# One persistent ring of four weight tiles, and fixed places for the first FFN matmul's operands

## The chip, the cores and the metric

The kernel runs on one core of one Trainium2 chip. The metric is the device time of one execution in microseconds. The figure before is a median of three runs; the trace is of one further execution, taken with the hardware profiler.

## The reference, cut to what is computed

A trunk of two layers on a stream `h` of 1024 frames by 1024 channels, all in fp32. Layer 0 mixes by a gMLP, layer 1 by attention over a band of chunks. Each is followed by a squared-ReLU MLP with 4096 hidden channels, and both halves stand between two RMS norms.

```
for layer in range(DEPTH):                       # DEPTH = 2
    g = norm_g[layer]
    if layer < N_A_LAYERS:                       # layer 0
        m = gmlp_spatial_gating(rms_norm(h, g[0]), ...)
    else:                                        # layer 1
        k_band, v_band, valid = shared_kv_band(h, kv_norm_g, w_k, w_v)
        m = chunk_band_attention(rms_norm(h, g[0]), ...)
    h = h + rms_norm(m, g[1])
    f = sq_relu_mlp(rms_norm(h, g[2]), w_up[layer], w_down[layer])
    h = h + rms_norm(f, g[3])

def sq_relu_mlp(h, w_up, w_down):
    return jnp.square(jax.nn.relu(h @ w_up)) @ w_down
```

## The kernel before

**Precision.** Each fp32 matmul is made of three: a value is split into a high part H (a CAST by ScalarE) and a low part L (value minus H, a subtraction by VectorE), `split`, L112 to L117, and `mm3` (L135 to L138) issues H·H, H·L and L·H. So each weight block that TensorE (PE) multiplies goes first through one ScalarE (ACT) instruction at L116 and then one VectorE (DVE) instruction at L117.

**First FFN matmul.** `ffn` walks over 16 pairs of 128 hidden channels, j = 0 to 15. A pair's weights come in two raw tiles of 128x1024 (`load_pair`; up12r and up28r for j = 12), four 128x512 blocks b11, b21, b12, b22. Pairs 0 to 2 use plain products (`plain`). From j = 3 on `blocks` does seven products of 4·3 matmuls in the place of eight: b11·z11, t2·s2, b21·z12, t1·s1, t3·z21, t4·z22, b22·s4. Here t1 to t4 are sums of weight blocks, z11 to z22 the quarters of the normed stream and s1, s2, s4 sums of these. While block j multiplies, `Prep` (L521 to L550) makes the split operands of pair j+1 in six steps, which `blocks` calls at written places between the products. This part is under `tc.manual_schedule`: all engines run it in the order in which the code is written. So a row of ACT or DVE in this part waits for the one written before it, whatever it belongs to.

Between the steps, `blocks` turns products into results: the sums into `left.u` and `left.at(1)` (L576, L592, L593, L599, L606 on DVE), relu and square on ACT (`squared`, L446 and L447), five sums of the results on GpSimd (POOL; `sums`, L455), and the spill of them to DRAM (`spill`, L461, issued by SyncE, SP). The last of the DVE sums of a block, L606, with its relu, square and POOL sums, is kept back (`finish`) until the next block has begun. PE's last product of a block, b22·s4, adds into the PSUM tile that L593 has read; so b22·s4 can't start before L593 is done.

The split operands are tiles of a ring `u` with 8 places. The raw weight tiles are a ring of two (`raw`): the second raw tile of a pair takes the place that the last split of step 5 frees.

**Second FFN matmul.** Seven products p over eight steps jj (`operands`, `mms`). `operands(p, jj)` loads a tile `xr` of spilled results and one or two weight tiles `xw` and splits both: r or hlx, and dn or hlx (L685, with `halves`). Four of eight such tiles lie in a ring `w` of four, the other four in hlx. Here the order on each engine is a scheduler's. Before this matmul, the last block's `before.finish()` is called behind `operands(0, 0)`, and `before.spill()` at jj = 1.

**The rings in SBUF.** Each stage opens its own group of 8 KB weight tiles on the right side of SBUF, and closes it: l0w and l1w (`w` by 4) for the gMLP, the projections and the second layer's projection; up0 and up1 (`u` by 8, the same bytes) for the first FFN matmul; dn0 and dn1 (`w` by 4) for the second; and the attention's wq, wk, wv, and v2 by 2. The quarters of z lie in tiles a0 to a3, taken from a pool of their own.

## Time and profile before

| | us |
|---|---|
| median of 3 runs | 2229.82 |
| lowest and highest | 2229.69, 2232.67 |
| the profiled execution | 2224.22 |
| its span | 2222.5 |
| PE busy | 2151.9 (97%) |
| DVE, ACT, POOL busy | 1497.9, 1050.8, 596.5 |
| mean granted clock of PE | 0.99 |

The profiled execution is 5.6 us shorter than the median; 1.7 us of it lie outside the span. PE is busy nearly all the time, so the stages' time is PE's work, the stretches in which PE's clock is granted at half, and some 60 us in which PE waits. What a change off PE does is read from those waits: which engine ends them, and where. Times in the rows are us from the start of the span.

### The profile page before, as it was taken

Reading aid. Unit: us, or ns where it says so; the run is one execution under the profiler, and the core shown is the slowest. Engines: PE = TensorE matmul, PEld = TensorE weight load, DVE = VectorE, ACT = ScalarE, POOL = GpSimd, SP = SyncE. Lnnn points to the kernel's source line nnn. Section 1 sums busy time; section 2 is a strip of 40 time slices with the busy share of each in tenths; the row PEclk is TensorE's granted clock in tenths of the full one; section 3 lists DMA queues with packets and bytes.
Section 4 is the critical chain, followed back from the end, with each engine's and each line's share of the span. In section 5 each row is a group of like instructions: output and inputs, shape, how many; then the busy total and the mean of one; then the engine's idle time right before and its main releaser. Section 6 shows DMA issues by size and latency. Waiting matters only on the chain. (4 is left out here: it accounts for less than half of the span.)

```text
span 2222.5 us, 26708 instructions
## 1 busy us (share of the span) xinstructions
PE 2151.9 (97%) x9848; PEld 1744.8 (79%) x9848; DVE 1497.9 (67%) x2214; ACT 1050.8 (47%) x1755; POOL 596.5 (27%) x395
## 2 busy tenths in 40 slices
PE   8999999999999999989999999999999999999997
PEld 6888778777778888867888888777877777788786
DVE  6745187666656677767888888766956665664477
ACT  5333254444444444555566566654534444533342
POOL 1000010333333553461111111201023333444343
PEclk9999999999999999999999999999999999999998
DMA  4121342444467887831111111154334344877775
GB/s 171 44 80 61 117 175 86 162 135 139 157 240 274 285 301 247 277 133 50 51 51 41 51 50 50 63 185 146 110 137 133 138 156 163 323 259 262 270 261 213
DMA packets 113508, 347.01 MB, mean 156 GB/s; under 512 B 11360, under 2 KB 11360, under 8 KB 113376
## 3 DMA queue, kind: packets, MB, share of 16 engines
q1 hardware_dynamic: 112224, 341.11, 43.9%
q0 software_dynamic: 1152, 4.19, 0.6%
q8 instruction: 77, 1.26, 0.2%
q14 instruction: 55, 0.45, 0.1%
HBM read 261.89 MB, written 83.36 MB: 155 GB/s over the span
## 5 line engine op out<-in xcount | busy, mean ns | idle before, releaser
L697 POOL TENSOR_TENSOR xw<-xw,xw 128x1024 f32<-128x1024 f32 x80 | 212.2, 2654 | 284.2 <-DMA xw<-in_w_dn 269.6
L137 PE MATMUL pd<-hlx 128*128 128x512 f32 x448 | 176.2, 393 | 7.0 <-DVE hlx L117 7.0
L137 PE MATMUL pd<-dn,r 128*128 128x512 f32 x448 | 178.4, 398 | 3.7 <-DVE dn L117 3.7
L136 PE MATMUL pd<-dn,r 128*128 128x512 f32 x448 | 175.9, 395 | 2.5 <-ACT dn L116 2.5
L138 PE MATMUL pd<-dn,r 128*128 128x512 f32 x448 | 177.6, 396 | 0.0
L136 PE MATMUL pd<-hlx 128*128 128x512 f32 x448 | 175.5, 392 | 1.3 <-ACT hlx L116 1.3
L138 PE MATMUL pd<-hlx 128*128 128x512 f32 x448 | 175.6, 392 | 0.0
L136 PE MATMUL pu<-z,b 128*128 128x512 f32 x400 | 159.2, 398 | 1.8 <-ACT po L148 1.8
L138 PE MATMUL pu<-z,b 128*128 128x512 f32 x400 | 158.4, 396 | 2.6 <-DVE b L117 2.6
L137 PE MATMUL pu<-z,b 128*128 128x512 f32 x400 | 158.0, 395 | 0.0
L117 DVE TENSOR_TENSOR r<-xr,r 128x1024 fp32r<-128x1024 f32 x56 | 97.6, 1744 | 73.5 <-ACT r L116 73.4
L117 DVE TENSOR_TENSOR hlx<-xr,hlx 128x1024 fp32r<-128x1024 f32 x56 | 91.6, 1636 | 67.2 <-ACT hlx L116 67.0
L1015 ACT ACTIVATE p<-p,mn 128x640 f32<-128x640 f32 (+4 forms) x128 | 89.2, 697 | 58.6 <-DVE mn L1010 57.4
L116 ACT CAST tH<-ptr 128x512 fp32r<-128x512 f32 x192 | 80.8, 421 | 68.6 <-PE ptr L1033 66.2
L117 DVE TENSOR_TENSOR tL<-ptr,tH 128x512 fp32r<-128x512 f32 x192 | 92.2, 485 | 27.3 <-ACT tH L116 26.1
L116 ACT CAST hlx<-xr 128x1024 fp32r<-128x1024 f32 x56 | 58.8, 1050 | 106.0 <-DMA xr<-r 75.0
L137 PEld LDWEIGHTS pd<-hlx 128*128 128x128 f32 x448 | 84.6, 189 | 27.6 <-DVE hlx L117 9.5
L116 ACT CAST r<-xr 128x1024 fp32r<-128x1024 f32 x56 | 58.6, 1047 | 99.5 <-PE pd L138 59.6
L137 PEld LDWEIGHTS pd<-dn,r 128*128 128x128 f32 x448 | 85.9, 192 | 24.0 <-DVE dn L117 5.8
L136 PEld LDWEIGHTS pd<-dn,r 128*128 128x128 f32 x448 | 85.1, 190 | 21.6 <-ACT dn L116 3.4
L138 PEld LDWEIGHTS pd<-dn,r 128*128 128x128 f32 x448 | 85.9, 192 | 18.2
L136 PEld LDWEIGHTS pd<-hlx 128*128 128x128 f32 x448 | 84.7, 189 | 19.6 <-ACT hlx L116 1.7
(563 smaller groups left out, 6031.4 us busy)
## 6 DMA issues: line engine op xcount, KB each, us to landing
xw<-in_w_dn SPq DMA_DIRECT2D x192, 512.0 KB, 4.7
xr<-r SPq DMA_DIRECT2D x112, 512.0 KB, 4.6
r<-rx SPq DMA_DIRECT2D x48, 512.0 KB, 3.9
r<-r SPq DMA_DIRECT2D x48, 512.0 KB, 3.8
h<-h SPq DMA_DIRECT2D x24, 512.0 KB, 5.1
h<-in_x SPq DMA_DIRECT2D x16, 512.0 KB, 3.5
h<-m SPq DMA_DIRECT2D x16, 512.0 KB, 2.7
braw<-in_rel SPq DMA_DIRECT2D x16, 320.0 KB, 4.6
```

The costliest lines, as they stand in the source:

```text
L116: nc.scalar.copy(dstH, src)
L117: (eng_l or nc.vector).tensor_sub(dstL, src, dstH.bitcast(F32))
L136: nc.tensor.matmul(ps, aH, bH, start=first, stop=False, **kw)
L137: nc.tensor.matmul(ps, aH, bL, start=False, stop=False, **kw)
L138: nc.tensor.matmul(ps, aL, bH, start=False, stop=last, **kw)
L697: nc.gpsimd.tensor_tensor(ws[0], ws[0], ws[1], op=op)
L1015: nc.scalar.activation(pt[:, :w], pt[:, :w], AF.Exp, bias=mn, scale=-1.0, accum_out=sm)
```

## The change

Four 8 KB tiles, two of a tag `wa` and two of a tag `wb`, are laid once for the whole kernel between the quarters a0, a1 and a2, a3, in a group g0. They take the place of l0w, l1w, up0, up1, dn0, dn1, the attention's wq, wk, wv and one of its two v2. In the first FFN matmul the operands get fixed places in these tiles: b11 and t3 share one, b21 and t4 one, t2 and t1 one, and two generations of b22 one. `Prep`'s steps change with it: t2 is made at the end of step 1 (was: the start of step 2), t1 in step 3 (was t3), t3 in step 4 (was t4), t4 in step 5 (was t1). The first block (j = 3) runs steps 3 and 4 ahead of t2's product and step 5 behind it. In the last block, `operands(0, 0)` of the second matmul is issued inside `blocks`, ahead of the relu and square of L594, and `before.finish()` directly behind the block. The tags of the other stages follow.

```
+    ctx.enter_context(ph.group("g0", [("wa", [P, 2, D], 2), ("a0", QUAD, 1), ("a1", QUAD, 1),
+                                      ("wb", [P, 2, D], 2), ("a2", QUAD, 1), ("a3", QUAD, 1)]))
+    W4 = ("wa", "wa", "wb", "wb")
...
     def proj_first(src, w, m_dst):
-        units = [load_unit(w[0, kp], f"wo0{kp}") for kp in range(4)]
+        units = [load_unit(w[0, kp], f"wo0{kp}", W4[kp]) for kp in range(4)]
...
+        wt = [ph.t(W4[i], f"wt{i}", dt=F32R).rearrange("p a (s c) -> p a s c", s=2) for i in (0, 2, 1, 3)]
+        places = {n: wt[i][:, a] for i, ns in enumerate((("b11", "t3"), ("b21", "t4"), ("t2", "t1"), ("b220", "b221")))
+                  for a, n in enumerate(ns)}
+
         def operand(name, src):
-            u = ph.t("u", name, dt=F32R)
+            u = places[name]
             split(u[:, 0], u[:, 1], src)
             return u
...
                     self.make("b22", b22)
                     v(b12, b22, b12)
                     v(b22, b22, b11)
+                    self.make("t2", b22)
                 elif i == 2:
-                    self.make("t2", b22)
                     self.make("b21", b21)
                 elif i == 3:
                     v(b21, b22, b21)
+                    self.make("t1", b11)
+                elif i == 4:
                     self.make("t3", b12)
-                elif i == 4:
+                elif i == 5:
                     self.make("t4", b21)
-                elif i == 5:
-                    self.make("t1", b11)
...
             if first:
                 s3_in_place()
                 prep.step(3)
+                prep.step(4)
             else:
                 before.finish()
                 step(0)
             product(b2, w["t2"], s2, **part)
             v(left.u[:, 0], left.t1, b2, op=OP.add)
             if first:
-                prep.step(4)
                 prep.step(5)
...
             v(left.at(1), left.u[:, 1], b3, op=OP.add)
+            if nxt is None:
+                ahead.append(operands(0, 0))
             left.squared(1, 1)
...
                 before = blocks(prep, nxt, before)
                 prep = nxt
-        yield
+            before.finish()
...
-                rw = operands(p, jj)
-                if p == 0 and jj == 0:
-                    before.finish()
+                rw = ahead.pop() if ahead else operands(p, jj)
                 if p == 0 and jj == 1:
                     before.spill()
...
-                self.v = ph.t("v2", f"v{p}", [P, NT, 2, 2, 64], F32R)
+                self.v = ph.t("wb" if p % 2 else "v2", f"v{p}", [P, NT, 2, 2, 64], F32R)
...
-                                         tag="w" + kind, scale=cols[:, 1 if kind == "q" else 2])
+                                         tag="wb" if kind == "k" else "wa", scale=cols[:, 1 if kind == "q" else 2])
```

In the order of instructions the rows move at three places. (In the rows shown the changed kernel's lines L119 to L464 are the lines L116 to L461 of before; its L633 and L637 are L691 and L695.)

First, ACT in a block of the first matmul in layer 0 (block 8, which prepares pair 9). Before, b22 and t2 are the names b229 and t29, and r82 and r80 are results of block 8:

```order
300 L116 CAST b119_3662<-up9r_3633 128x512
301 L116 CAST b229_3679<-up25r_3635 128x512
302 L446 ACTIVATE r82_3640<-pu81_3642 128x512
303 L447 ACTIVATE r82_3640<-r82_3640 128x512
304 L116 CAST t29_3698<-up25r_3635 128x512
305 L116 CAST b219_3701<-up9r_3633 128x512
306 L116 CAST t39_3718<-up25r_3635 128x512
307 L446 ACTIVATE r80_3638<-r80_3638 128x512
308 L447 ACTIVATE r80_3638<-r80_3638 128x512
```

The changed kernel at the same place (wt0 to wt3 are the four shared tiles; wt3 holds b22, wt1 t2 and t1, wt2 b21):

```order
300 L119 CAST wt0_2357<-up9r_3594 128x512
301 L119 CAST wt3_2360<-up25r_3596 128x512
302 L119 CAST wt1_2359<-up25r_3596 128x512
303 L449 ACTIVATE r82_3601<-pu81_3603 128x512
304 L450 ACTIVATE r82_3601<-r82_3601 128x512
305 L119 CAST wt2_2358<-up9r_3594 128x512
306 L119 CAST wt1_2359<-up9r_3594 128x512
307 L449 ACTIVATE r80_3599<-r80_3599 128x512
308 L450 ACTIVATE r80_3599<-r80_3599 128x512
```

The CAST of t2 has moved ahead of the relu and square of r82, and so b21's CAST stands directly behind these; t1 has taken t3's turn.

Second, SP at the start of layer 0's second matmul. r07<-rx are the four spills of the last block, xr and xw loads of the second matmul. Before:

```order
154 L461 DMA r07_2341<-rx_2342 128x2x512 x2
155 L461 DMA r07_2341<-rx_2342 128x512
156 L691 DMA xr02_4839<-r02_2336 128x1024
157 L695 DMA xw020_4841<-in_w_dn 128x1024
158 L461 DMA r07_2341<-rx_2342 128x2x512
```

The changed kernel:

```order
152 L464 DMA r07_2352<-rx_2353 128x2x512
153 L633 DMA xr02_4747<-r02_2347 128x1024
154 L464 DMA r07_2352<-rx_2353 128x2x512
155 L464 DMA r07_2352<-rx_2353 128x512
156 L464 DMA r07_2352<-rx_2353 128x2x512
157 L637 DMA xw020_4749<-in_w_dn 128x1024
```

The load xw020 has moved behind the last spill of the block; xr02 has moved ahead of three of the spills.

Third, DVE at the start of layer 1's first matmul. b110 to b220 are the split operands of pair 0, m5 to m7 and z the end of the projection ahead of it. Before:

```order
1752 L142 TENSOR_SCALAR pri6_13322<-pss6_13320 128x1
1753 L209 TENSOR_TENSOR z32_12889<-ztr3_1_13305,z32_12889 128x4x128
1754 L213 SCALAR_TENSOR_TENSOR m6_13271<-m6_13271,pri6_13322,gpost_12901 128x1024
1755 L214 TENSOR_TENSOR m6_13271<-m6_13271,h6_13273 128x1024
1756 L142 TENSOR_SCALAR zri5_13331<-zss5_13329 128x1
1757 L197 SCALAR_TENSOR_TENSOR m5_13206<-m5_13206,zri5_13331,gnext_12903 128x1024
1758 L117 TENSOR_TENSOR b110_13389<-up0r_13385,b110_13389 128x512
1759 L117 TENSOR_TENSOR b210_13392<-up0r_13385,b210_13392 128x512
1760 L117 TENSOR_TENSOR b120_13395<-up16r_13387,b120_13395 128x512
```

The changed kernel, in which wt0 takes the high and low parts of pair 0's b11:

```order
1752 L145 TENSOR_SCALAR pri6_13214<-pss6_13212 128x1
1753 L212 TENSOR_TENSOR z32_12784<-ztr3_1_13197,z32_12784 128x4x128
1754 L216 SCALAR_TENSOR_TENSOR m6_13163<-m6_13163,pri6_13214,gpost_12793 128x1024
1755 L120 TENSOR_TENSOR wt0_13271<-up0r_13277,wt0_13271 128x512
1756 L217 TENSOR_TENSOR m6_13163<-m6_13163,h6_13165 128x1024
1757 L145 TENSOR_SCALAR zri5_13223<-zss5_13221 128x1
1758 L120 TENSOR_TENSOR wt1_13273<-up0r_13277,wt1_13273 128x512
1759 L120 TENSOR_TENSOR wt2_13272<-up16r_13279,wt2_13272 128x512
1760 L120 TENSOR_TENSOR wt3_13274<-up16r_13279,wt3_13274 128x512
```

The subtraction for pair 0's b11 has moved ahead of m6's addition and of m5's scaling, the other three ahead of m5's scaling.

## Rows read from the trace of the kernel before

**Rows 1.** The page's part 1: busy us, share, instructions of each engine.

```profile
PE 2151.9 (97%) x9848; PEld 1744.8 (79%) x9848; DVE 1497.9 (67%) x2214; ACT 1050.8 (47%) x1755; POOL 596.5 (27%) x395
```

**Rows 2.** Windows: stretch, length, busy PE, PEld, DVE, ACT, POOL; clock, DMA, GB/s.

```profile
428.53:628.12 199.59, 197.73 (x840) 156.86 (x840) 130.03 (x160) 93.24 (x160) 72.84 (x50) 1.00 0.44 148
1670.14:1869.96 199.82, 198.72 (x841) 157.01 (x841) 129.16 (x160) 93.24 (x161) 72.86 (x50) 1.00 0.43 145
650.70:660.70 10.00, 7.06 (x19) 5.24 (x19) 9.53 (x6) 6.08 (x8) 7.17 (x4) 0.66 0.90 315
1892.60:1899.80 7.20, 4.25 (x12) 3.10 (x12) 7.12 (x5) 5.12 (x7) 6.88 (x4) 0.76 0.91 318
1265.00:1272.00 7.00, 5.26 (x30) 4.33 (x29) 5.71 (x14) 3.75 (x11) 4.21 (x4) 1.00 0.19 75
```

**Rows 3.** Waits of PE in 415 to 640: us in total, times, longest.

```profile
PE pu L136 <- DVE r L593: 1.4, 6, 0.2
```

**Rows 4.** Timeline of ACT in a block: start, length, what, [idle before <-releaser].

```profile
556.72 0.63 ACT L447 ACTIVATE u<-u 128x512 f32<-128x512 f32 x1
557.26 0.60 ACT L116 CAST b<-up12r 128x512 fp32r<-128x512 f32 x1
559.54 0.62 ACT L116 CAST b<-up28r 128x512 fp32r<-128x512 f32 x1 [1.68 <-DMA up28r<-in_w_up]
560.07 0.59 ACT L446 ACTIVATE rx<-pu 128x512 f32<-128x512 f32 x1
560.69 0.63 ACT L447 ACTIVATE rx<-rx 128x512 f32<-128x512 f32 x1
...
563.54 0.62 ACT L116 CAST t<-up28r 128x512 fp32r<-128x512 f32 x1 [2.21 <-DVE up28r L540]
564.07 0.62 ACT L116 CAST b<-up12r 128x512 fp32r<-128x512 f32 x1
```

**Rows 5.** Timeline of DVE in the same block.

```profile
554.05 1.38 DVE L117 TENSOR_TENSOR t<-up11r,t 128x512 fp32r<-128x512 f32 x1 [1.87 <-ACT t L116]
...
559.61 1.36 DVE L536 TENSOR_TENSOR up12r<-up28r,up12r 128x512 f32<-128x512 f32 x1 [0.34 <-DMA up28r<-in_w_up]
...
564.80 0.69 DVE L117 TENSOR_TENSOR b<-up12r,b 128x512 fp32r<-128x512 f32 x1
...
567.44 0.69 DVE L593 TENSOR_TENSOR rx<-u,pu 128x512 f32<-128x512 f32 x1
```

**Rows 6.** Timeline of SP's queue in the same block: when the load was issued.

```profile
555.45 0.33 SPq L406 DMA_DIRECT2D up28r<-in_w_up  x1
```

**Rows 7.** Timeline of PE where four stages start or hand over.

```profile
651.97 1.20 PE L136 MATMUL pd<-dn,r 128*128 128x512 f32 x4 [1.23 <-ACT dn L116]
...
1497.86 0.50 PE L136 MATMUL po<-wo,o 128*128 128x512 f32 x1 [0.72 <-ACT ms L238]
...
1555.86 0.50 PE L138 MATMUL pu<-z,b 128*128 128x512 f32 x1 [2.55 <-DVE b L117]
...
1567.61 1.03 PE L193 MATMUL ztr<-ident,m 128*128 128x128 f32 x8
```

**Rows 8.** Timeline of DVE at the start of layer 1's first matmul.

```profile
1550.58 1.28 DVE L213 SCALAR_TENSOR_TENSOR m<-m,pri,gpost 128x1024 f32<-128x1024 f32 x1
...
1566.70 1.29 DVE L117 TENSOR_TENSOR b<-up1r,b 128x512 fp32r<-128x512 f32 x2 [0.52 <-ACT b L116]
```

**Rows 9.** Timeline at layer 0's second matmul: two rows of DVE, one each of POOL, SP.

```profile
651.38 1.22 DVE L117 TENSOR_TENSOR r<-xr,r 128x1024 fp32r<-128x1024 f32 x1
652.51 2.31 DVE L117 TENSOR_TENSOR dn<-xw,dn 128x1024 fp32r<-128x1024 f32 x1
...
655.92 2.26 POOL L455 TENSOR_TENSOR rx<-u,rx 128x512 f32<-128x512 f32 x1
...
658.20 0.37 SPq L461 DMA_DIRECT2D r<-rx  x1
```

**Rows 10.** The page's part 6: loads of xw, count, KB, median us to landing.

```profile
xw<-in_w_dn SPq DMA_DIRECT2D x192, 512.0 KB, 4.7
```

More of the change, by code (lines that the diff above doesn't have):

```diff
@@ L241, in proj_first @@
     def proj_first(src, w, m_dst):
-        units = [load_unit(w[0, kp], f"wo0{kp}") for kp in range(4)]
+        units = [load_unit(w[0, kp], f"wo0{kp}", W4[kp]) for kp in range(4)]
         ps = {}
@@ L267, in proj_second @@
         tail = Tail(zn, g_post, g_next, h_dst, first)
-        units = [load_unit(w[1, kp], f"wo1{kp}") for kp in range(4)]
+        units = [load_unit(w[1, kp], f"wo1{kp}", W4[kp]) for kp in range(4)]
         if rest is not None:
@@ L368, in run_ffn @@
         f = ffn(layer, *a)
-        before[0].__exit__(None, None, None)
-        with ExitStack() as dn:
-            with ph.group(f"up{layer}", [("u", [P, 2, 512], 8)], side="right"):
-                next(f)
-                next(proj, None)
-                before[1].__exit__(None, None, None)
-                dn.enter_context(ph.group(f"f{layer}", [("ps", [P, 512], 8)], **PS))
-                ph.live["tr"] = ph.live["ps"]
-                next(f)
-            dn.enter_context(ph.group(f"dn{layer}", [("w", [P, 2, D], 4)], side="right"))
+        next(f)
+        next(proj, None)
+        before.__exit__(None, None, None)
+        with ph.group(f"f{layer}", [("ps", [P, 512], 8)], **PS):
+            ph.live["tr"] = ph.live["ps"]
             for _ in f:
@@ L408, in load_pair @@
             return r
+        wt = [ph.t(W4[i], f"wt{i}", dt=F32R).rearrange("p a (s c) -> p a s c", s=2) for i in (0, 2, 1, 3)]
+        places = {n: wt[i][:, a] for i, ns in enumerate((("b11", "t3"), ("b21", "t4"), ("t2", "t1"), ("b220", "b221")))
+                  for a, n in enumerate(ns)}
         def operand(name, src):
-            u = ph.t("u", name, dt=F32R)
+            u = places[name]
             split(u[:, 0], u[:, 1], src)
@@ L528, in make @@
             def make(self, name, src):
-                self.w[name] = operand(f"{name}{self.j}", src)
+                self.w[name] = operand(name + str(self.j % 2) if name == "b22" else name, src)
             def step(self, i):
@@ L540, in step @@
                     v(b22, b22, b11)
+                    self.make("t2", b22)
                 elif i == 2:
-                    self.make("t2", b22)
                     self.make("b21", b21)
@@ L571, in blocks @@
                 prep.step(3)
+                prep.step(4)
             else:
@@ L593, in blocks @@
             v(left.at(1), left.u[:, 1], b3, op=OP.add)
+            if nxt is None:
+                ahead.append(operands(0, 0))
             left.squared(1, 1)
@@ L611, in blocks, with halves, operands, plain_operands @@
             return left
-        def plain_operands(j, src):
+        made, hlx, ahead = [0], {}, []
+        def halves(raw, name):
+            n = made[0] % 8
+            made[0] += 1
+            i = n // 2
+            if n >= 4 and i not in hlx:
+                hlx[i] = quad(i, f"hlx{i}", F32R)
+            d = ph.t(W4[n], name, [P, 2, T], F32R) if n < 4 else hlx[i][:, n % 2 * 2:n % 2 * 2 + 2]
+            split(d[:, 0], d[:, 1], raw)
+            return [d[:, i].rearrange("p (a c) -> p a c", a=2) for i in range(2)]
+        def operands(p, jj):
+            place, terms, op, _ = PRODUCTS[p]
+            raw = ph.t("raw", f"xr{p}{jj}")
+            nc.sync.dma_start(raw, r_dram[jj][:, place * T:(place + 1) * T])
+            ws = []
+            for i, (kh, dh) in enumerate(terms):
+                ws.append(ph.t(wtags[i % len(wtags)], f"xw{p}{jj}{i}"))
+                nc.sync.dma_start(ws[-1], wdn[kh, dh, jj])
+            if op is not None:
+                nc.gpsimd.tensor_tensor(ws[0], ws[0], ws[1], op=op)
+            return halves(raw, f"r{p}{jj}"), halves(ws[0], f"dn{p}{jj}")
+        def plain_operands(src, names):
             b11, b21, b12, b22 = src
-            w = [operand(f"b11{j}", b11), None, operand(f"b21{j}", b21), None]
-            w[1], w[3] = operand(f"b12{j}", b12), operand(f"b22{j}", b22)
-            return w
+            w = [operand(n, x) for n, x in zip(names, (b11, b21, b12, b22))]
+            return [w[0], w[2], w[1], w[3]]
+        own = ("t3", "t1", "t4", "b220"), ("b11", "t2", "b21", "b221")
         with tc.manual_schedule(engines=ALL):
-            w0 = plain_operands(0, load_pair(0))
+            w0 = plain_operands(load_pair(0), own[0])
         yield
@@ L673, in ffn @@
                 prep = nxt
[L674 removed]
+            before.finish()
         acc = [quad(i, f"acc{i}", F32) for i in range(2)]
[L676 to L698 removed]
         def mms(ps, tt, jj, rw):
@@ L725, in ffn @@
             for jj in range(n):
-                rw = operands(p, jj)
-                if p == 0 and jj == 0:
-                    before.finish()
+                rw = ahead.pop() if ahead else operands(p, jj)
                 if p == 0 and jj == 1:
@@ L828, in gmlp @@
             v_tile(0, t, units)
-        units = [load_unit(io["w_inv"][1, kp], f"wv1{kp}", tag="w" if kp else "x") for kp in range(4)]
+        units = [load_unit(io["w_inv"][1, kp], f"wv1{kp}", tag=W4[kp] if kp else "x") for kp in range(4)]
         for t in range(NT):
```

80 lines of the change are left out of this document (28 added, 52 removed).

## The prediction

> **What bounds the kernel now.** I read the page's first part, then windows, then the waits and timelines of the places that the change touches. PE is busy 97% of the span [rows 1]: the reader is to see that nothing which saves work off PE saves time unless PE waits for it. So the question is where PE waits, and who ends the wait.
>
> In blocks 4 to 14 of the first FFN matmul, the longest stretch that the change touches, PE is busy 197.73 of 199.59 us in ten blocks of layer 0 and 198.72 of 199.82 in layer 1 [rows 2]. That is one block in 19.96 and 19.98 us, of which PE idles 0.19 and 0.11. It idles always at one place, ahead of b22·s4, for DVE's L593 [rows 3]. So a loop that doesn't contain PE has the same period as PE, to 0.2 us. The loop can be followed in one block. Step 5's last split, 554.05 + 1.38, frees a raw tile [rows 5]; the load of up28r is issued at 555.45 [rows 6]; DVE's L536 starts at 559.61, let go by that load [rows 5]; from there ACT and DVE hand each other the splits until L593, 567.44 to 568.13 [rows 4, 5]; behind L593 come the relu and square, and steps 4 and 5 with the next such split. No row of ACT or DVE on this path waits for PE: ACT waits for DVE, for a DMA and for L540. The loop runs by itself, and has no slack to give.
>
> **The change part by part.**
>
> *The order in Prep's steps.* ACT's wait of 2.21 us ahead of t2's CAST, for L540 [rows 4], is now filled with the relu and square of the running block (560.07, 560.69). The change puts t2's CAST ahead of them, as the two ACT listings show. They can't start before L540 is done then, and b21's CAST, which followed t2's by 0.53 (563.54 to 564.07), follows behind them. Starts on ACT: CAST to relu 0.53 (559.54 to 560.07), relu to square 0.62 (560.07 to 560.69), square to CAST 0.54 (556.72 to 557.26), together 1.69 [rows 4]. b21's CAST comes 1.69 - 0.53 = 1.16 later. DVE's subtraction for it started 0.73 behind the CAST's start (564.07 to 564.80), 0.11 more than the CAST's 0.62 [rows 4, 5], I suppose because DVE was still busy; it won't be now, so between 1.05 and 1.16 reach DVE. I take 1.08. From that subtraction to L593 DVE's rows stand back to back, 564.80 to 567.44 = 2.64 [rows 5], and their number and form stay (t1's low part for t3's). So L593 comes 1.08 later in each block; nothing else of the loop gets shorter, since step 5 still ends with a split from the same raw tile and the load still waits for it. The period becomes 21.04 in layer 0. The eleven blocks 4 to 14 prepare a next one: 11 x 1.08 = **+11.9 us**. In layer 1 the loop stands 0.08 nearer to PE's own period (0.11 idle for 0.19), so I take 1.0: 11 x 1.0 = **+11.0**. Upper end 22 x 1.16 = +25.5. The cover of the old order was ACT's 2.21 us wait; with it gone, nothing else hides the two instructions. Lower end: nothing, if the loop doesn't hold PE (a rival). Each block then has a wait of some 1.3 us ahead of b22·s4.
>
> *The start of layer 0's second matmul.* PE waits there 1.23 us for dn's CAST [rows 7]; in the window 650.70 to 660.70 it idles 10.00 - 7.06 = 2.94 in all, and the granted clock is 0.66, which costs another 0.34 x 10 = 3.4 [rows 2]. The change issues r00 and dn00 before the block's end, beside t4·z22 and b22·s4, and could remove most of 6.3. But xw020 now stands on SP behind the last spill of the block (SP listings). That spill waits for POOL's last sum, 655.92 + 2.26, and went at 658.20 [rows 9]; with the relus and squares behind the CASTs of r00, dn00 and r01 I put it at some 660. The load takes 4.7 [rows 10], the subtraction 1.22 [rows 9] and the CAST ahead of it about as much, so dn02 is there at 667 at the earliest. PE, without its first waits, would be through jj = 0 and 1 (2 x 24 matmuls of 197.73 / 840 = 0.235 [rows 2], 11.3 us) at 651 + 11.3 = 662.3. It waits 4 to 6 us at jj = 2, and the clock falls again. Before, with 6.3 lost, it came there at 650.7 + 6.3 + 11.3 = 668.3. So the gain is given back: between -6 (xw020 in time) and +6 (the longer wait costs clock twice); I take **+2**.
>
> *The start of layer 1's second matmul.* The same waits: idle 7.20 - 4.25 = 2.95, clock 0.76, 0.24 x 7.2 = 1.7, in all 4.65 [rows 2]. Here xw020 stands ahead of the spills. I keep 0.3 of wait for dn00: **-4.3**, between -4.65 and -2.
>
> [...] The row first: a subtraction of 128x1024 takes 1.22 in one row and 2.31 in the next, around POOL's sums [rows 9]. [...] The splits of r00 and dn00 move among POOL's sums of the last block. [...]
>
> *The start of layer 1's first matmul.* PE waits 2.55 for b11's low part [rows 7], which stood on DVE behind m6's and m5's instructions. Now it follows L213, which ends at 1550.58 + 1.28 = 1551.86 [rows 8], so it is there at some 1552.5, when PE is. The next pair's splits at 1566.70 [rows 8] move only some 0.6 earlier, and PE, which came to them behind the transposes at 1567.61 + 1.03 [rows 7], would come 2.55 earlier: up to 0.6 of the gain is lost there. **-2.0**, between -2.55 and 0.
>
> *The projection ahead of it.* wo1's tiles now share wa with two of wo0, and are filled only when those are read. PE's wait there is 0.72 now [rows 7]; I estimate **+1.0**, between 0 and +2 (a load's 4.7 [rows 10] less what the remaining tiles cover).
>
> *The rest.* Block 3's steps and the attention's shared tags move loads and splits whose next use lies later than the move; +0.3 in all, between -2 and +2.
>
> Sum: 11.9 + 11.0 + 2 - 4.3 - 2.0 + 1.0 + 0.3 = **+19.9 us**. On the profiled execution that is 2224.2 + 19.9 = 2244.1. The median of the runs lies 5.6 above it; the same difference on the median gives 2249.7, and I forecast 2250.
>
> **The rivals.** (1) *The loop doesn't hold PE.* If PE paces the loop (L593 waits for PE's own sums, say, by an amount under what the rows resolve), 1.08 is paid once in each layer: 2.2 - 3.0 of the rest = -0.8, 2229. For it: PE's idle in the blocks is under 1% [rows 2]. Against: DVE runs without a break into L593, and the wait is there in more than half of the blocks. (2) *The same, and xw020 comes in time.* Then layer 0's start gives -6: 2.2 - 3.0 - 8 = -8.8, **2221**, faster. It decides by whether the spill goes before 655, since the load and the split then end by 662. Against: POOL's last sum starts no earlier than before. (3) *Each new wait makes the clock fall.* A fall as in the window at 1892.60 costs 1.7 [rows 2]; a block that runs late by 1.7 has no wait at b22·s4, so about every second block pays, part of it inside the loop's slack: +5 to +37, 2255 to 2287. Against: the window 1265 to 1272 holds 1.74 us of idle PE and its clock is 1.00 [rows 2]. [...] (4) *The change doesn't do what it says*: the shared tiles could make a CAST of one operand wait for PE's reading of its neighbour in the tile. b11's CAST would then wait for t3·z21, some 8 us in a block (from 557.26 to just ahead of L592 and L593 [rows 4, 5]), and the time would go beyond 2300. The order gives b11's CAST no PE to wait for; I hold it for very unlikely.
>
> **How the numbers follow.** The forecast has 0.70, rival 1 0.10, rival 2 0.12, rival 3 0.06, rival 4 0.02. With the terms at their lower ends together (17 - 6 - 4.65 - 2.55 - 2, with 17 from 0.78 a block, if the loop has 0.3 of slack that the rows don't show) the forecast's case reaches +2; at its upper ends (25.5 + 6 - 2 + 0 + 2 + 2) +33. Ends don't meet, so +9 to +29 holds most of it. To hold 8 in 10 the range takes in rival 1's neighbourhood and a part of rival 3: 2231 to 2262, the forecast's own being 2239 to 2259. A measurement of this kernel can tell about 0.2%, 4.5 us. Faster: rival 2 and a tail, 0.13. Same: rival 1 and the forecast's lowest ends, 0.12. Slower: 0.75.
>
> **What would show it.** Right: PE waits near 1.3 us ahead of b22·s4 in blocks 4 to 14, ended by L593, the period 21.0; ACT's relu of the running block directly behind t2's CAST; no wait of PE at layer 1's two starts; in layer 0 a wait at jj = 2 behind xw020. Wrong: a period that stays at 20.0, or b21's CAST that comes no later. The half clock inside the blocks would bear out rival 3; a wait of ACT for PE at b11's CAST rival 4.

## The result, and the profile after

The changed kernel is slower: 2246.15 us, median of six runs (2243.9 to 2249.81), against 2230.01 before (2229.69 to 2232.67, six runs). The ratio is 1.0071, with an interval of [1.0058, 1.0084]: 16.1 us more. The profiled execution took 2244.61, its span is 2242.8; that of before took 2224.22. So the two profiles stand 20.4 apart and the medians 16.1, because the profile of before lies 5.8 below its median and that of after 1.5.

The first part of the page of after (busy time, share of the span, instructions), which answers to [rows 1]:

```profile
PE 2133.7 (95%) x9848; PEld 1748.3 (78%) x9848; DVE 1510.0 (67%) x2214; ACT 1049.1 (47%) x1755; POOL 598.2 (27%) x395
```

PE has 18 us less of busy time than before, with the same number of matmuls, in a span that is 20 longer. Two things have happened, in opposite directions, and only one of them was forecast.

Stretches of after: from:to, length, busy PE (matmuls), PEld, DVE, ACT and POOL, clock, DMA share, GB/s. The first two run over ten blocks, from the last product of block 4 to that of block 14, in layers 0 and 1, and answer to the ten-block windows of [rows 2]. The next two, called the starts of the second FFN matmul below, hold the last block and the first 96 matmuls of the second FFN matmul, and the last lies in the gMLP:

```profile
425.11:635.92 210.81, 196.07 (x840) 157.01 (x840) 130.87 (x160) 93.10 (x160) 72.82 (x50) 1.00 0.42 140
1687.52:1898.93 211.41, 196.95 (x841) 159.16 (x841) 130.81 (x160) 92.92 (x161) 72.73 (x50) 0.98 0.41 137
635.92:686.58 50.66, 46.42 (x192) 37.10 (x193) 25.04 (x23) 24.72 (x31) 14.25 (x10) 0.97 0.68 241
1898.93:1944.22 45.29, 45.29 (x192) 37.29 (x193) 24.55 (x21) 22.93 (x30) 15.23 (x10) 0.96 0.69 244
100.00:260.00 160.00, 159.99 (x774) 134.29 (x774) 69.43 (x75) 50.93 (x67) 2.24 (x4) 1.00 0.24 75
```

The last three of them in the trace of before, the same pieces of work (the gMLP window is the same time):

```profile
628.12:678.63 50.51, 47.57 (x192) 37.99 (x193) 27.42 (x23) 24.49 (x32) 15.83 (x10) 0.93 0.76 268
1869.96:1919.23 49.27, 46.33 (x193) 37.05 (x193) 27.03 (x23) 24.04 (x31) 16.79 (x11) 0.97 0.76 267
100.00:260.00 160.00, 160.00 (x761) 131.94 (x760) 68.74 (x77) 49.23 (x65) 3.75 (x5) 1.00 0.21 68
```

The reader is to see three things. A block of the first matmul now takes 21.08 and 21.14 us, for 19.96 and 19.98. The start of the second matmul is 4 us shorter in layer 1 and no shorter in layer 0. And in the gMLP, whose order of work did not change, PE does 774 matmuls in 160 us where it did 761.

Cut at PE's instructions, the two profiles differ so (us, after less before):

| stretch | before | after | difference | forecast |
|---|---|---|---|---|
| start to layer 0's first FFN matmul | 313.01 | 308.27 | -4.7 | 0 |
| layer 0, block 3 to block 14 | 221.08 | 233.53 | +12.5 | +11.9 |
| layer 0, start of the second matmul | 50.51 | 50.66 | +0.2 | +2 |
| start of the attention | 28.5 | 31.6 | +3.1 | 0 |
| layer 1, projection | 54.73 | 55.59 | +0.9 | +1.0 |
| layer 1, first matmul to block 3 | 96.20 | 96.29 | +0.1 | -2.0 |
| layer 1, block 3 to block 14 | 221.17 | 234.59 | +13.4 | +11.0 |
| layer 1, start of the second matmul | 49.27 | 45.29 | -4.0 | -4.3 |
| the rest | | | -1.1 | +0.3 |
| sum | | | +20.4 | +19.9 |

**One block after.** ACT, start, length, what, [idle before <-releaser]; block 12 of layer 0, which answers to [rows 4]. The CASTs are b22's (584.10), t2's (588.04), and b21's together with t1's (589.73); L449 and L450 are the relu and square of the running block:

```profile
584.10 0.62 ACT L119 CAST wt<-up29r 128x512 fp32r<-128x512 f32 x1 [1.84 <-DMA up29r<-in_w_up]
588.04 0.62 ACT L119 CAST wt<-up29r 128x512 fp32r<-128x512 f32 x1 [3.32 <-DVE up29r L543]
588.57 0.59 ACT L449 ACTIVATE r<-pu 128x512 f32<-128x512 f32 x1
589.19 0.63 ACT L450 ACTIVATE r<-r 128x512 f32<-128x512 f32 x1
589.73 1.12 ACT L119 CAST wt<-up13r 128x512 fp32r<-128x512 f32 x2
```

DVE behind it, which answers to [rows 5]; the three rows are the low parts of t2 and b21, and L596 (L593 of before):

```profile
588.70 0.69 DVE L120 TENSOR_TENSOR wt<-up29r,wt 128x512 fp32r<-128x512 f32 x1 [0.74 <-ACT wt L119]
590.36 0.69 DVE L120 TENSOR_TENSOR wt<-up13r,wt 128x512 fp32r<-128x512 f32 x1 [0.98 <-ACT wt L119]
...
593.02 0.69 DVE L596 TENSOR_TENSOR r<-u,pu 128x512 f32<-128x512 f32 x1
```

And PE's b22·s4, with the waits of PE in 415 to 640 (us in total, times, longest), which answer to [rows 3]:

```profile
593.76 0.50 PE L139 MATMUL pu<-s,wt 128*128 128x512 f32 x1 [1.54 <-DVE r L596]
```

```profile
PE pu L139 <- DVE r L596: 8.1, 6, 1.5
PE pu L139 <- DVE rx L596: 7.1, 5, 1.4
```

From t2's CAST to b21's it is 589.73 - 588.04 = 1.69, the 1.69 that the prediction summed from ACT's starts, where it was 0.53. From b21's subtraction to L596 it is 593.02 - 590.36 = 2.66 (forecast 2.64). PE waits 15.2 us in eleven blocks, 1.4 each, always at this place.

### The profile page after: what moved, and what is told of

It is laid out like the page before. It is cut to its first block, busy times and chain, and to the rows that moved or that the text cites. A ratio compares the mean times of both kernels' runs of the same rounds, so it can differ in the third digit from the quotient of the medians.

```text
span 2242.8 us, 26750 instructions
## 1 busy us (share of the span) xinstructions
PE 2133.7 (95%) x9848; PEld 1748.3 (78%) x9848; DVE 1510.0 (67%) x2214; ACT 1049.1 (47%) x1755; POOL 598.2 (27%) x395
## 5 line engine op out<-in xcount | busy, mean ns | idle before, releaser
L639 POOL TENSOR_TENSOR xw<-xw,xw 128x1024 f32<-128x1024 f32 x80 | 218.1, 2727 | 274.3 <-DMA xw<-in_w_dn 247.5
L139 PE MATMUL pu<-z,wt 128*128 128x512 f32 x608 | 239.2, 393 | 2.4 <-ACT po L151 2.3
L141 PE MATMUL pu<-z,wt 128*128 128x512 f32 x608 | 237.3, 390 | 0.9 <-DVE wt L120 0.9
L140 PE MATMUL pu<-z,wt 128*128 128x512 f32 x608 | 238.0, 391 | 0.0
L140 PE MATMUL pd<-dn,r 128*128 128x512 f32 x448 | 174.9, 390 | 0.3 <-DVE dn L120 0.3
L139 PE MATMUL pd<-dn,r 128*128 128x512 f32 x448 | 175.0, 391 | 0.0
L141 PE MATMUL pd<-dn,r 128*128 128x512 f32 x448 | 174.8, 390 | 0.0
L139 PE MATMUL pu<-s,wt 128*128 128x512 f32 x312 | 128.6, 412 | 43.8 <-DVE rx L596 24.7
L139 PEld LDWEIGHTS pu<-z,wt 128*128 128x128 f32 x608 | 114.9, 189 | 28.1 <-ACT po L151 2.6
L141 PEld LDWEIGHTS pu<-z,wt 128*128 128x128 f32 x608 | 114.6, 189 | 25.8 <-DVE wt L120 1.3
L140 PEld LDWEIGHTS pu<-z,wt 128*128 128x128 f32 x608 | 114.8, 189 | 23.8
L141 PE MATMUL pu<-s,wt 128*128 128x512 f32 x312 | 126.0, 404 | 3.6 <-DVE wt L120 3.6
L140 PE MATMUL pu<-s,wt 128*128 128x512 f32 x312 | 125.8, 403 | 0.0
L120 DVE TENSOR_TENSOR dn<-xw,dn 128x1024 fp32r<-128x1024 f32 x56 | 89.4, 1596 | 42.6 <-ACT dn L119 42.1
L120 DVE TENSOR_TENSOR hlx<-xw,hlx 128x1024 fp32r<-128x1024 f32 x56 | 89.0, 1589 | 35.6 <-ACT hlx L119 35.4
L139 PEld LDWEIGHTS pu<-s,wt 128*128 128x128 f32 x312 | 60.5, 194 | 66.6 <-DVE rx L596 29.8
```

The lines of the kernel that those rows point to most:

```text
L120: (eng_l or nc.vector).tensor_sub(dstL, src, dstH.bitcast(F32))
L139: nc.tensor.matmul(ps, aH, bH, start=first, stop=False, **kw)
L140: nc.tensor.matmul(ps, aH, bL, start=False, stop=False, **kw)
L141: nc.tensor.matmul(ps, aL, bH, start=False, stop=last, **kw)
L639: nc.gpsimd.tensor_tensor(ws[0], ws[0], ws[1], op=op)
```

## The experiments

The lines of the changed kernel are three higher than those of before in `split` and `blocks` (L596 is L593).

### Does the place of t2 cost the time of the blocks?

First the change with t2 put back to the start of step 2, all else left:

```
                     v(b22, b22, b11)
-                    self.make("t2", b22)
                 elif i == 2:
+                    self.make("t2", b22)
```

> The changed kernel with one line moved back: t2 is made at the start of step 2 again, so on ACT the relu and square of the running block stand ahead of t2's CAST; ring, fixed places and early operands(0, 0) stay. Theory A (the order in Prep is the cost): the period of blocks 4 to 14 falls from 21.1 back to 20.0, 22 blocks by 1.1 to 1.2 = 25, time 2246 - 25 = 2221 (2217 to 2225), below the kernel before. Rival B (the cost lies in the shared tiles or in the moved steps 3 to 5): the period stays near 21 and the time above 2240.

Measured: 2218.53, ratio 0.995 [0.9934, 0.9966], faster than before by 12 us and than the change by some 27. Then the other way round: the kernel before, with nothing but t2 at the end of step 1.

```
                     v(b22, b22, b11)
-                elif i == 2:
                     self.make("t2", b22)
+                elif i == 2:
```

> The kernel before with that one line alone: t2 at the end of step 1. Theory A: 22 x 1.08 to 1.16 = 24 to 26 more than before, 2254 to 2256, with PE waiting 1.2 ahead of b22*s4 in each block. Rival B: no change, 2230.

Measured: 2253.49, ratio 1.0104 [1.0087, 1.0122], 22.6 us slower. The ten blocks of layer 0, the window of t2 put back first, then that of t2 alone:

```profile
425.04:624.63 199.59, 196.19 (x840) 156.98 (x840) 129.60 (x160) 93.24 (x160) 72.79 (x50) 1.00 0.44 148
```

```profile
431.45:642.29 210.84, 197.78 (x840) 156.88 (x840) 130.97 (x160) 93.06 (x160) 72.80 (x50) 1.00 0.42 140
```

The one line moves the block from 19.96 to 21.08 and back, in either kernel. That settles the main term: the rest of the change neither causes nor needs it. It also leaves a gain of some 12 us in the rest of the change, more than the prediction had there.

### Why is PE faster in the gMLP?

Start to start, the 128x512 matmuls of the two products with z take a median of 227 ns there, for 233 to 234 before (the window holds smaller matmuls too). The ring stood between the quarters now, so the first theory (L) was the ring's place. The experiment lays the ring behind all four quarters:

```
-    ctx.enter_context(ph.group("g0", [("wa", [P, 2, D], 2), ("a0", QUAD, 1), ("a1", QUAD, 1),
-                                      ("wb", [P, 2, D], 2), ("a2", QUAD, 1), ("a3", QUAD, 1)]))
+    ctx.enter_context(ph.group("g0", [("a0", QUAD, 1), ("a1", QUAD, 1), ("a2", QUAD, 1), ("a3", QUAD, 1),
+                                      ("wa", [P, 2, D], 2), ("wb", [P, 2, D], 2)]))
```

> The changed kernel with the four tiles laid behind all four quarters of z instead of between them; nothing else differs. In the trace after the change PE runs 774 matmuls in 100 to 260 us, before 761. Theory L (the pace comes from where the tiles lie): here 761 again, the first FFN matmul starts some 5 us later (313 for 308), and the rest of layer 1's projection too; the blocks are held by the loop, so little there: 2246 + 5 to 10 = 2251 to 2256. Rival: the pace comes from something else in the change (which tiles are shared, the order of splits): 774 stays, 2246.

Measured: 2248.52, ratio 1.0083 [1.0062, 1.0105], and in the gMLP window still 774 matmuls:

```profile
100.00:260.00 160.00, 160.00 (x774) 134.37 (x773) 69.46 (x75) 50.94 (x67) 3.56 (x5) 1.00 0.23 74
```

The time alone does not tell this run from the change, whose interval overlaps; the count does. The theory fell. What the ring does have in both places is the start address of its tiles: by the layout of the programs they stand alike with the quarters modulo 256 bytes of a partition, and in the kernel before they do not. No profile shows an address, so the differences given here are read from the layout, and what the runs vary is the pads. Three pads of 32 bytes, between ring and quarters, undo that, and move the tiles behind them as well:

```
+    pad = [P, 8]
+    ctx.enter_context(ph.group("g0", [("wa", [P, 2, D], 2), ("pad0", pad, 1), ("a0", QUAD, 1), ("a1", QUAD, 1), ("pad1", pad, 1),
+                                      ("wb", [P, 2, D], 2), ("pad2", pad, 1), ("a2", QUAD, 1), ("a3", QUAD, 1)]))
...
```

> The changed kernel with three pads of 32 bytes a partition between the ring's tiles and the quarters of z, so that the ring starts at a multiple of 64 bytes and the quarters (and all tiles behind them) at 32 more; nothing else differs. In the traces so far matmuls whose two operands start alike modulo 64 bytes follow each other at 227 ns, others at 232 to 234 (before: ring at 32, z at 0). Theory M (the pace comes from this): the window 100 to 260 holds 761 matmuls again in the place of 774, the first FFN matmul of layer 0 starts at some 313 in the place of 308, and with the projection of layer 1 and the plain blocks the time is 2246 + 7 to 11 = 2253 to 2257. Rival (the pace comes from the tiles' distance or order): 774 and 2246.

Measured: 2255.83, ratio 1.0123 [1.0103, 1.0144], 10 us slower than the change, and 760 matmuls in the window:

```profile
100.00:260.00 160.00, 160.00 (x760) 132.11 (x759) 68.36 (x76) 49.29 (x65) 2.79 (x5) 1.00 0.21 68
```

The other way round, the kernel before with one pad of 32 bytes under its right side, which makes ring and quarters alike modulo 64:

```
+    ctx.enter_context(ph.group("g1", [("padr", [P, 8], 1)], side="right"))
+    ph.t("padr", "padr")
```

> The kernel before with one pad of 32 bytes at the top of the right side, so that its rings start at a multiple of 64 bytes as the quarters of z do. Theory M: 774 matmuls in 100 to 260, first FFN matmul of layer 0 at some 308 for 313, the blocks 4 to 14 keep their period of 20.0, since the loop of splits and loads holds it, and PE's wait ahead of b22*s4 grows from 0.2 to some 0.6: 2230 - 5 to 10 = 2220 to 2225. Rival: 761 and 2230.

Measured: 2227.66, ratio 0.999 [0.9978, 1.0002]: 1.1 us less, not told from none, where 5 to 10 were expected. The window has 768 matmuls, half of the way. The starts still differ by 64 modulo 256. So the kernel before was padded once more, 224 bytes on the right and 128 at the left of each stage's group, which makes them all alike modulo 256:

```
+    ctx.enter_context(ph.group("g1", [("padr", [P, 56], 1)], side="right"))
...
-    with ph.group("l0", [("raw", full, 2), ("x", full, 2), ("st2", full, 2), *quad[2:], ("st", full, 3), ("row", full, 2)]):
+    with ph.group("l0", [("padl", [P, 32], 1), ("raw", full, 2), ("x", full, 2), ("st2", full, 2), *quad[2:], ("st", full, 3), ("row", full, 2)]):
```

> The kernel before with pads of 224 bytes on the right side and of 128 bytes ahead of each stage's own tiles, so that its rings and the quarters start alike modulo 256 bytes. In e6 (alike modulo 64 only) the matmuls of layer 0's first FFN matmul came to 229 to 230 ns, those of layer 1's stayed at 233. Theory M' (alike modulo 256): 227 in both, 774 matmuls in 100 to 260, layer 0's first FFN matmul at some 308, blocks 4 to 14 still 20.0 a block, since the loop holds them: 2229 - 5 to 9 = 2220 to 2224. Rival (modulo 64 is all there is, or the pace hangs on something else): 768 or less, 2226 or more.

Measured: 2217.59, ratio 0.9945 [0.9925, 0.9966], 12 us faster than before (5 to 9 expected) by bytes that nothing reads. First its gMLP window and the ten blocks of layer 0, then the gMLP window of the pad of 32:

```profile
100.00:260.00 160.00, 159.88 (x775) 134.66 (x774) 69.02 (x75) 50.94 (x68) 3.16 (x4) 1.00 0.24 77
421.10:621.33 200.23, 193.74 (x841) 156.82 (x841) 128.73 (x160) 93.25 (x160) 72.80 (x50) 1.00 0.44 147
```

```profile
100.00:260.00 160.00, 160.00 (x768) 133.54 (x767) 69.23 (x77) 49.77 (x66) 3.68 (x5) 1.00 0.21 70
```

| kernel | ring and quarters, difference of starts modulo 256 | matmuls in 100 to 260 |
|---|---|---|
| before | 32 | 761 |
| after | 0 | 774 |
| ring behind the quarters | 0 | 774 |
| after, pads of 32 | 32 or 96 | 760 |
| before, pad of 32 | 64 | 768 |
| before, pads of 224 and 128 | 0 | 775 |

The padded kernel's blocks still take 20.0 us though PE is busy 4 us less in ten of them: there the loop of load and splits sets the pace.

### How much does that loop hold?

The loop runs from step 5's last split over the load into the raw tile it frees. On top of t2 put back, step 5 was moved ahead of the running block's sum, relu and square, so that the load can go earlier:

```
             product(b4, w["t4"], z22)
+            if not first:
+                step(5)
             v(left.u[:, 1], left.u[:, 1], b4, op=OP.subtract)
             left.squared(1, 0)
             left.sums(5, 6)
-            step(*(4, 5) if first else (5,))
+            if first:
+                step(4, 5)
```

> e1 with one more edit: step 5 of Prep (t4's split, which frees the raw tile for the next load) directly behind t4*z22, ahead of L602's subtraction, relu and square. Theory A' (the loop of splits, load and L593 holds PE; the load is issued when step 5 is done): the load is issued some 3 us earlier in each block, the loop is shorter than PE's own work, PE's wait ahead of b22*s4 goes, the period falls to PE's 84 x 0.227 to 0.230 = 19.1 to 19.4, 22 x 0.7 = 15 less than e1: 2206 (2202 to 2212). Rival: the load isn't what holds the loop, or t4's CAST waits for PE's reading of the old t4: as e1, 2221.

Measured: 2203.08, ratio 0.9874 [0.9855, 0.9893], another 15.5 us. In 415 to 630 PE waits once for L596, 0.8 us. The ten blocks in layers 0 and 1:

```profile
425.62:618.87 193.25, 193.25 (x841) 157.88 (x842) 126.15 (x160) 94.27 (x162) 68.73 (x50) 1.00 0.45 153
1673.06:1863.60 190.54, 190.54 (x841) 157.77 (x841) 126.47 (x160) 94.04 (x162) 69.31 (x50) 1.00 0.45 152
```

PE is busy without a gap, 19.33 and 19.05 us a block. Layer 0 is the slower one; I put that down to its s1 to s4, which lie elsewhere, 96 off from the ring modulo 256, and the last version below, which pads these 96 bytes, has 19.06 in layer 0. The same move in the kernel before:

> The kernel before with one edit: step 5 of Prep (there t1's split) directly behind t4*z22, as in e4. Theory A' (the loop from step 5's load to L593 holds PE): the loop gets some 3 us shorter, PE's own 84 matmuls at 234 ns = 19.7 hold the block, period 19.7 for 19.97, 22 x 0.25 = 5.5 less: 2224 (2221 to 2226). Rival: the period of 20.0 is PE's own: 2229.

Measured: 2218.48, ratio 0.9951 [0.9936, 0.9966], 11 us faster; I had expected half of that. The ten blocks of layer 0:

```profile
430.31:625.55 195.24, 195.24 (x840) 157.75 (x841) 126.71 (x160) 93.36 (x162) 68.94 (x50) 1.00 0.46 153
```

A block takes 19.52 us there, so the loop had held PE back by 0.44 us a block, where 0.19 was shown as idle [rows 2]. The other 0.25 stood in the busy time: 197.73 in ten blocks before, 195.24 here, for the same 840 matmuls. Both edits together, pads and step 5, in the kernel before:

> e10 and e11 together. Theory (both limits must go, the loop's 19.97 and PE's 234 ns): period 84 x 0.227 to 0.230 = 19.1 to 19.3, 22 x 0.75 = 16 less in the blocks, and e10's 5 to 9 outside them: 2229 - 23 = 2206 (2202 to 2210), more than e10's and e11's gains added. Rival: the gains just add, 2215 to 2219.

Measured: 2199.47, ratio 0.9858 [0.9838, 0.9878], 30 us faster (23 expected), where the two alone gave 12 and 11. The block takes 19.05:

```profile
422.06:612.59 190.53, 190.53 (x840) 157.82 (x841) 127.24 (x160) 93.02 (x161) 69.39 (x50) 1.00 0.47 155
```

That is the mark of two limits that lie close together, PE's pace (19.5) and the loop's (20.0): lifting one alone only reaches the other.

### The starts of the second matmul: is it the early call?

The change without the early `operands(0, 0)`, and with `finish` behind it as before; the ring stays:

```
-            if nxt is None:
-                ahead.append(operands(0, 0))
...
-            before.finish()
...
-                rw = ahead.pop() if ahead else operands(p, jj)
+                rw = operands(p, jj)
+                if p == 0 and jj == 0:
+                    before.finish()
```

> The changed kernel without the early operands(0, 0) of the second FFN matmul: they are issued behind the last block, and finish() behind them, as before the change. Theory: layer 1's start loses its 4.0 again (PE waits of 1.2 and 1.7 for dn, and the half clock behind them); layer 0's start, where the early operands were given back at jj = 2 (wait of 3.45 for xw020), stays within 1: 2246 + 4 = 2250. Rival (the early operands gain nothing, or the gain came from the faster matmuls): 2246.

Measured: 2239.0, ratio 1.0052 [1.003, 1.0073]. I had expected it to be slower than the change, and it is not; the intervals overlap, so the stage has to tell. The two starts, layers 0 and 1:

```profile
639.16:683.79 44.63, 44.28 (x193) 36.08 (x193) 23.01 (x20) 21.46 (x29) 16.25 (x10) 1.00 0.76 257
1901.80:1945.73 43.93, 43.93 (x192) 36.08 (x193) 25.77 (x22) 23.95 (x31) 16.22 (x10) 1.00 0.77 266
```

44.63 and 43.93, for 50.66 and 45.29 in the change and 50.51 and 49.27 before. So the gain at the starts comes with the ring, and without the call the scheduler itself takes the splits of r00 and dn00 ahead into the last block. The moved t2 is not the reason: PE in the kernel before with t2 alone still waits 1.2 and 1.7 us for dn there, in both layers. That the old order waited for a group to be closed and opened is argued from the code; no run separates it from the other things that the ring changes. Some of the 5 to 6 us is the faster matmul: its median goes from 230 and 231 ns to 227, and 192 times that is, by my estimate, 0.6 to 0.8. The early call adds nothing, and in layer 0 it costs. SP's queue in the change, then without the early call; L464 is a spill, L637 and L635 are the load of xw020:

```profile
660.06 0.38 SPq L464 DMA_DIRECT2D r<-rx  x1
...
662.31 5.10 SPq L464 DMA_DIRECT2D r<-rx  x3
667.50 0.42 SPq L637 DMA_DIRECT2D xw<-in_w_dn  x1
```

```profile
661.91 0.37 SPq L464 DMA_DIRECT2D r<-rx  x1
662.38 0.42 SPq L635 DMA_DIRECT2D xw<-in_w_dn  x1
664.16 2.55 SPq L464 DMA_DIRECT2D r<-rx  x2
```

With the early call the load waits for three more spills, and these for POOL's sums (SP waits 12.1 us for them in 655 to 670, 6.9 at the longest). It goes 5 us later, and 8.4 later counted from the start of the stretch (635.92 and 639.16).

### The start of the attention

In the change, the CAST of wk1, the next pair's keys, stands on ACT ahead of L317, a step of the norm for whose result PE waits; and it waits itself, 3.41 us, for POOL's scaling of the loaded tile:

```profile
994.61 1.04 ACT L119 CAST wk<-wk1r 128x1024 fp32r<-128x1024 f32 x1 [3.41 <-POOL wk1r L133]
995.56 1.14 ACT L317 ACTIVATE acc<-acc,pri 128x1024 f32<-128x1024 f32 x1
```

In the trace of before no CAST of wk1 stands in that stretch. The experiment gives pair 1's keys the other tag, whose tiles come free later:

```
-                                         tag="wb" if kind == "k" else "wa", scale=cols[:, 1 if kind == "q" else 2])
+                                         tag="wb" if kind == "k" and self.p != 1 else "wa", scale=cols[:, 1 if kind == "q" else 2])
```

> The changed kernel with one tag changed: the attention's wk of pair 1 takes a wa tile, for which it has to wait, instead of the free wb tile. In the changed kernel's trace its CAST stands on ACT ahead of the scaling (L317) of tile 6 and waits 3.4 for POOL, and PE then waits 6.2 and 1.2 at 993 to 1002. Theory W (this early split delays the last transposes): its CAST goes behind the scalings, PE's waits there return to some 4.1 and 0.6 as before, 2 to 5 less: 2241 to 2244. Rival (the waits come from z's chain itself): 2246.

Measured: 2241.37, ratio 1.0053 [1.0036, 1.007]. PE's waits for z at that place, in 979 to 1011, first in the change and then here; before they are 4.7, with a longest of 4.1:

```profile
PE ztr L157 <- DVE z L120: 7.4, 2, 6.2
```

```profile
PE ztr L157 <- DVE z L120: 5.9, 1, 5.9
```

No CAST of wk1 stands there any more, and the wait shrinks by 1.5 of the 2.7 that the change added. The stretch itself takes 30.6, for 31.6 in the change and 28.5 before, so 1.0 of the 3.1 is given back. The median falls by more, but its interval overlaps that of the change. The rest of the 3.1 stays open.

### A version that beats both kernels

Together: the change with t2 put back, step 5 early, no early call, pair 1's keys in `wa`, the first block's steps 3 and 4 ahead of `s3_in_place`, and 96 bytes of padding on the right, so that layer 0's s tiles too are alike modulo 256.

```
+    ctx.enter_context(ph.group("g1", [("padr", [P, 24], 1)], side="right"))
+    ph.t("padr", "padr")
...
             if first:
-                s3_in_place()
                 prep.step(3)
                 prep.step(4)
+                s3_in_place()
```

> e4 (t2 back in step 2, step 5 early) with four more edits: no early operands(0, 0) (as e8), pair 1's wk in a wa tile (as e7), in the first block the splits of steps 3 and 4 ahead of s3's splits, and a pad of 96 bytes on the right side, which brings layer 0's s tiles to the ring's offset modulo 256 bytes. Theory: each takes its own wait, and the sums add: e4 2203, less 6 to 7 (layer 0's wait at jj = 2 and its half clock), 2 to 4 (attention's start), 3 to 8 (block 3's wait of 5 to 7 in each layer, as far as the raw tile is freed earlier), 1 to 2 (s products of layer 0 from 234 to 227 ns): 2188 (2182 to 2197). Rival (they hide one another): 2200 or more.

Measured: 2185.1, median of five runs (2182.7 to 2185.51), ratio 0.9795 [0.9781, 0.9809]: 45 us faster than before and 61 faster than the change. The ten blocks of layer 0 take 19.06 us each, with PE busy throughout, and from 560 to 700, over the start of the second matmul, no wait of PE is shown:

```profile
420.94:611.51 190.57, 190.57 (x840) 157.76 (x841) 127.69 (x160) 94.19 (x162) 69.21 (x50) 1.00 0.46 155
```

It stands 14 us below the best that the old rings gave (2199.47). The two starts of the second matmul are the largest piece of that which the runs show. From the last product of block 14 on, the same 204 matmuls take 52.67 and 49.80 us in the kernel of 2199.47, whose matmuls are as fast, and 46.24 and 46.47 here: 9.8 us in all. So the ring is worth having once the order is right. What the other edits of this version give by themselves was not run.

## Why the prediction was right, step by step

The forecast was 2250 and slower; 2246.15 lies 3.9 below it, in its own range and on its side.

**The sum: partly luck.** From profile to profile +19.9 was forecast and +20.4 measured, but the terms were further off than that. By the table the blocks came out 3.0 above, the start of the attention 3.1 and layer 1's first matmul 2.1; PE's pace ahead of the first FFN matmul came out 4.7 below, layer 0's second matmul 1.8 and the rest 1.4. With two smaller ones these errors cancel to 0.5. What carries the forecast is the main term.

**The blocks: right, in mechanism and nearly in size.** 22 times 1.08 or 1.0 was 22.9, measured 25.9 (12.5 and 13.4). The cover named, ACT's wait ahead of t2's CAST, was the right one, and b21's CAST came later by the 1.16 worked out; 1.12 of it reached the period in layer 0, a little above the 1.08 taken. The discount for layer 1 (1.0 for its smaller idle time) was wrong: 1.16 there. PE waits 16.4 us in eleven blocks of layer 1, and the granted clock of the ten is 0.98 for 1.00 in layer 0.

PE's waits in 1687 to 1899 of after (us in total, times, longest):

```profile
PE pu L139 <- DVE r L596: 11.0, 6, 1.9
PE pu L139 <- DVE rx L596: 5.4, 5, 1.7
```

The granted clock falls twice in these ten blocks, behind the two longest waits (1.95 us each, ended at 1687.52 and 1772.31), to 0.51 in the window below and to 0.50 in 1773.50 to 1776.70:

```profile
1688.10:1691.40 3.30, 3.30 (x9) 2.58 (x8) 2.02 (x2) 1.18 (x4) 1.28 (x1) 0.51 0.00 0
```

So there is a little of rival 3 in layer 1 and none of it in layer 0, where waits of up to 1.5 us leave the clock at 1.00. Not every new wait made the clock fall: in layer 1's ten blocks it fell behind these two only. Rivals 1 and 4 are out: the period rose by the whole step, and ACT's rows show no wait for PE.

**Layer 0's second matmul: the described wait, a smaller sum.** PE waits at jj = 2 behind xw020, as forecast, so rival 2 is out:

```profile
673.17 0.73 PE L139 MATMUL pd<-hlx 128*128 128x512 f32 x2 [3.45 <-ACT hlx L119]
674.43 0.79 PE L140 MATMUL pd<-hlx 128*128 128x512 f32 x1 [0.52 <-DVE hlx L120]
```

The stage begins 7.8 us later in after (635.92 for 628.12), and in those terms the steps held: xw020's load goes at 667.50 (forecast some 660 + 7.8), PE is through jj = 1 at 669.7 (662.3 + 7.8 = 670.1) and waits 4.0 there, at the low end of 4 to 6. What was mis-sized is the clock. I let it fall again and took a value between -6 and +6; the granted clock of the stage is 0.97, and 0.03 x 50.66 = 1.5 us is what that costs, where 0.07 x 50.51 = 3.5 was paid before (in 656.00 to 660.70 of before it was 0.50). Idle and clock together cost 4.2 + 1.5 now and 2.9 + 3.5 before, 0.7 less; measured is +0.2, for +2 forecast. The 0.9 between them is not accounted for; the clock, read to a hundredth, makes each of its two terms uncertain by 0.25.

The split of dn00 did not fall among POOL's sums, and did not take the 2.31 of [rows 9]: its subtraction took 1.23 (1.22 in layer 1) while POOL was idle. Where POOL's sums ran, the same form took 1.64 and 1.97 (in before 1.22 at 651.38 and 2.31 behind it, with POOL's sums from 650.17 to 653.75); what makes one longer than another, no run shows:

```profile
657.45 1.23 DVE L120 TENSOR_TENSOR dn<-xw,dn 128x1024 fp32r<-128x1024 f32 x1
...
661.72 1.64 DVE L120 TENSOR_TENSOR dn<-xw,dn 128x1024 fp32r<-128x1024 f32 x1
666.12 1.97 DVE L120 TENSOR_TENSOR hlx<-xr,hlx 128x1024 fp32r<-128x1024 f32 x1 [2.76 <-ACT hlx L119]
```

```profile
658.74 1.30 POOL L458 TENSOR_TENSOR rx<-rx 128x512 f32<-128x512 f32 x1 [11.13 <-ACT rx L450]
660.87 3.64 POOL L458 TENSOR_TENSOR rx<-u,rx 128x512 f32<-128x512 f32 x2 [0.84 <-POOL rx L458]
...
665.72 1.29 POOL L458 TENSOR_TENSOR rx<-u,rx 128x512 f32<-128x512 f32 x1
```

**Layer 1's second matmul: the size right by luck, the cause wrong.** -4.0 for -4.3. I gave it to the early call; the run without that call has an even shorter start (43.93). With the ring in place the splits go early without it. The step that failed is the reading of the old order: it took the place of `operands(0, 0)` in the code for what held dn00, and not something in the old rings, of which the group that had to be closed and opened is the likely part. The size is made of other terms, too. The 2.94 of idle PE is gone, as forecast, but the 1.7 for the clock is not given back, since the granted clock is 0.96 where it was 0.97: it falls behind a wait of 1.80 ahead of block 14's b22·s4, which the moved t2 makes.

```profile
1899.90:1903.10 3.20, 3.20 (x9) 2.44 (x8) 2.01 (x2) 1.12 (x3) 1.27 (x1) 0.50 0.19 72
```

The other 1.0 is busy time, 45.29 for 46.33, most of it by the faster matmuls.

**Layer 1's first matmul: wrong.** -2.0 was forecast, +0.1 came. b11's wait of 2.55 [rows 7] has become 0.89, but behind it the transposes wait 1.49, where they had not waited [rows 7], and in block 3 PE waits 1.50 for a split and 6.96 for L596, where it waited 1.3 and 2.0 for two splits:

```profile
1569.65 0.50 PE L141 MATMUL pu<-z,wt 128*128 128x512 f32 x1 [0.89 <-DVE wt L120]
...
1576.42 1.09 PE L196 MATMUL ztr<-ident,m 128*128 128x128 f32 x8 [1.49 <-DVE z L212]
...
1664.34 0.79 PE L139 MATMUL pu<-s,wt 128*128 128x512 f32 x1 [6.96 <-DVE rx L596]
```

The prediction asked whether the next pair's splits would give a part of the 2.55 back, but not whether the loop's first round, some 95 us later, would be ready any earlier. It is not, so a PE that comes earlier waits longer there. How much of the 6.96 is that, and how much the new order of the first block's steps, no run separates.

**The projection:** +0.9 for +1.0. **The rest** was put at +0.3 "in all". It holds two terms that it should have named: the attention's start, +3.1, of which wk1's tag explains 1.0, and PE's own pace, -4.7 ahead of the first FFN matmul (with the pads of 32 that matmul starts at 313.76 again, for 308.27 in the change and 313.01 before). For the second, the prediction took a matmul's 0.235 us as fixed by its shape; where tiles move, it was not (0.227 in the gMLP's products with z). In the blocks that gain is hidden by the loop.

**The offset.** The prediction put the forecast's profile 5.6 below its median, like that of before; it was 1.5. The profile forecast (2244.1 for 2244.61) was nearer than the median's (2249.7 for 2246.15): the step from the profile to the median is what nearly all of the 3.9 comes from.

## What to carry to other kernels

When a loop of load, split and free buffer runs at the pace of the bound engine, follow it instruction by instruction, in the order in which each engine runs them: here one instruction moved ahead of two that had filled a wait cost 1.12 and 1.16 us in each round. PE that is shown busy need not be PE at its best pace (774 matmuls for 761 in the same 160 us, busy in both), so before and after a move of tiles count matmuls in equal windows of a stage whose work did not change. And two limits close together have to be lifted together, or each of them looks worth little (12 and 11 us alone, 30 together).

## What was not expected of the hardware

In the gMLP's products with z, a matmul of 128x512 fp32 parts follows the last after a median of 227 ns in the change, where ring and quarters start alike modulo 256 bytes, and after 233 to 234 in the kernel before, where they differ by 32. In the same 160 us the kernels of the table have 774 or 775 matmuls where the starts are alike, 768 where they differ by 64, and 760 or 761 where they differ by 32 or 96, at a granted clock of 1.00 in all of them. Over the kernel it was worth 10 us in the change (2255.83 with the pads of 32) and 12 in the kernel before (2217.59 with those of 224 and 128). The difference is not all there is: the gMLP's last product, which reads v's tiles in another place, takes 231 ns in the change, and 233 before. Why it is so, no run here shows; nor were other differences tried by themselves.

A wait of PE's does not tell by its length alone whether the clock falls: in layer 1 of the change it fell behind one of 1.80 us (ended at 1898.93; 0.50 in 1899.90 to 1903.10) and not behind one of 1.81 (ended at 1856.77; 1.00 in 1856.77 to 1860.50). What decides it, no run here shows.
